# Feed-forward input products as seven block products (Strassen) for pairs of weight pieces

## The chip, the cores and the metric

The kernel runs on one core of a Trainium2 chip. TensorE (PE; PEld is its weight load) multiplies, VectorE (DVE), ScalarE (ACT) and GpSimd (POOL) do the elementwise work, and the queue of SyncE (SP) issues most transfers. The metric is device time in microseconds (us) of one launch, the median of several runs.

## The reference

One step of a two-layer model over 640 tokens (128 of context, 512 latent) with 1024 channels, all in fp32. Each layer has a token-mixing part (attention, neighbourhood attention and a Fourier branch, merged by gates) and a feed-forward part; both are modulated by vectors that come from `c` and `c_ctx`:

```python
mod = silu(c) @ w_ada[l] + b_ada[l]               # 6 x 1024 values: shifts, scales, gates
h = rms_norm(x, g_pre[1]) * (1 + sc2) + sh2       # 640 x 1024
g, u = split(h @ w_ffn_in[l], 2)                  # each 640 x 2816
x = x + g2 * rms_norm((silu(g) * u) @ w_ffn_out[l], g_post[1])
```

## The kernel before

**Products.** Every large product is made of three: each operand is split into a high part, rounded to TensorE's fp32r format, and a low part, the rest; high x high, high x low and low x high are summed in PSUM. The normalised input stands transposed in `hT_hi`, `hT_lo` (channels on partitions, 8 blocks of 128; 640 tokens along the free side).

**Weight pieces.** Weights come in pieces of 512 KB, `[128, 1024]`. A feed-forward input piece (kind `fg` for the gate, `fu` for the other half) holds 128 output channels of all 8 blocks of input channels. `Weights` walks the pieces in the order in which a dry run asked for them: `pump` issues the load of the next piece into one of four `wraw` buffers on SP's queue, `split_next` writes its high part with ACT (`whi`) and its low part with DVE (`wlo`) into one of three slots, and frees the `wraw` buffer.

**Feed-forward.** `ffn` handles the 22 blocks of 128 hidden channels in three parts of 6, 8 and 8 (`FFN_PARTS`). In a part, `proj2` takes each piece for two groups of tokens (384 and 256): 24 matmuls in each, then `evac`. For `fg` ACT takes a tanh and DVE makes `(tanh + 1) * g` in the tile `sg`; for `fu` DVE multiplies, ACT writes the high part into `aT` and DVE the low part. Then `xstat` multiplies `aT` by the output weights (`fo` pieces, 30 matmuls of 512 columns each) and adds into `y`; in the last part `xstat_tiles` does it and finishes one tile of tokens after another.

**Modulation.** The 12 rounds of `w_ada` (a layer, a sixth; 8 pieces of 512 KB each) are spread as a generator, of which `step` takes one tick for every `ada_dt` us of nominal matmul time. In the first layer's token mixing they are small matmuls on TensorE (`wraw,ada_st`, four for a piece). In the feed-forward (`acc` given) each piece is two DVE instructions on 1024 columns, and eight small matmuls with `ones` close a round: six rounds in layer 0 and one in layer 1, with `ADA_DT = 3.0`. `ada_finish` takes all ticks that are left, at once, ahead of the last part's `fo` products.

Each engine works through its own queue in the order in which this code writes it.

Of the kernel before, what the change touches and what calls it, by code (L numbers as in the profile page):

```python
# [69 lines left out]
class Unit:  # L70
    def __init__(self, key):
        self.key = key
        self.raw = self.hi = self.lo = None
        self.done = False


class Weights:
# [41 lines left out]
    def pump(self, bufs=RAW_BUFS):  # L121
        while self.n_dma < len(self.order) and self.n_dma < self.freed + bufs:
            u = self.units[self.order[self.n_dma]]
# [5 lines left out]

    def split_next(self):  # L130
        if self.n_split >= len(self.split):
            return False
# [11 lines left out]
        nc.scalar.activation(hi[:, :u.n], u.raw[:, :u.n], AF.Copy)  # L144
# [1312 lines left out]
```

## Time and profile before

| | us |
|---|---|
| median of 3 runs | 2192.57 (2192.06 to 2193.25) |
| the profiled execution | 2196.1, of which 2194.3 from its first to its last instruction |
| PE busy | 2156.5 (98%) |
| DVE busy | 1131.7 (52%) |
| ACT busy | 790.7 (36%) |
| POOL busy | 354.4 (16%) |

The profiled execution is 3.5 us above the median. A busy PE is not a PE at its peak, since the recorded matmuls overlap; what a matmul costs is read from a stage's time over its count. In the trace, layer 0's feed-forward runs from 645 to 1127 us and layer 1's from 1717 to 2187 us. The input products of their parts are the stretches 645 to 735, 777 to 893, 950 to 1066, and 1717 to 1807, 1849 to 1962, 2018 to 2131 us.

### The profile page before, as it was taken

To read this page: it belongs to the slowest core of one execution; us is meant where nothing else is said; L and a number is where in the kernel's file an instruction comes from. 1 tells how busy PE (TensorE), PEld (TensorE's weight loads), DVE (VectorE), ACT (ScalarE), POOL (GpSimd) and SP (SyncE) were. 2 spreads that over 40 slices of the span, in tenths; PEclk is the share of its full clock that TensorE was granted. 3 is DMA by queue.
4 is the path that set the end of the run, shared out by engine and by line. 5 is a ranking of instruction groups with operands and counts; after the bars stand their busy time and mean duration, and the time that the engine had idled before them with its cause. 6 is when DMAs were issued, how large, how long until landed. Compare 5 with 4: busy or idle time off the path is not lost. (4 is left out here: it accounts for less than half of the span.)

```text
span 2194.3 us, 35177 instructions
## 1 busy us (share of the span) xinstructions
PE 2156.5 (98%) x14260; PEld 2006.2 (91%) x14260; DVE 1131.7 (52%) x2025; ACT 790.7 (36%) x1640; POOL 354.4 (16%) x635
## 2 busy tenths in 40 slices
PE   6999999999999999999999999999999999999998
PEld 3999999998889899899879999999998898998996
DVE  3555565543366566666465556555533662333333
ACT  3644444432253222122256445444433522221221
POOL 2101223322131000000041013233111300000002
PEclk9999999999999999999999999999999999999999
DMA  7311223325634444443332113333124332222221
GB/s 270 109 56 51 63 75 87 83 75 168 237 87 160 136 138 138 146 148 107 107 107 84 49 58 69 82 82 86 60 72 144 108 105 77 77 77 71 74 88 67
DMA packets 250049, 223.78 MB, mean 102 GB/s; under 512 B 10016, under 2 KB 209728, under 8 KB 249632
## 3 DMA queue, kind: packets, MB, share of 16 engines
q1 hardware_dynamic: 243408, 209.60, 30.4%
q0 software_dynamic: 6048, 11.68, 2.6%
q8 instruction: 113, 1.85, 0.3%
q14 instruction: 48, 0.39, 0.1%
q10 hardware_dynamic: 432, 0.25, 0.0%
HBM read 214.91 MB, written 6.59 MB: 101 GB/s over the span
## 5 line engine op out<-in xcount | busy, mean ns | idle before, releaser
L487 PE MATMUL ps_mm<-hT_hi,whi 128*128 128x256 f32 (+1 forms) x2832 | 885.8, 313 | 1.5 <-DVE sg L1098 1.0
L489 PE MATMUL ps_mm<-hT_hi,wlo 128*128 128x256 f32 (+1 forms) x2832 | 877.6, 310 | 0.4 <-DVE wlo L145 0.4
L488 PE MATMUL ps_mm<-hT_lo,whi 128*128 128x256 f32 (+1 forms) x2832 | 877.0, 310 | 0.0
L487 PEld LDWEIGHTS ps_mm<-hT_hi,whi 128*128 128x128 f32 x2832 | 533.3, 188 | 10.7 <-issue 6.0
L489 PEld LDWEIGHTS ps_mm<-hT_hi,wlo 128*128 128x128 f32 x2832 | 533.2, 188 | 0.9 <-DVE wlo L145 0.9
L488 PEld LDWEIGHTS ps_mm<-hT_lo,whi 128*128 128x128 f32 x2832 | 533.3, 188 | 0.6
L145 DVE TENSOR_TENSOR wlo<-wraw,whi 128x1024 fp32r<-128x1024 f32 x253 | 312.8, 1237 | 390.7 <-ACT whi L144 390.1
L144 ACT ACTIVATE whi<-wraw 128x1024 fp32r<-128x1024 f32 x253 | 267.0, 1056 | 274.1 <-PE ps_mm L1138 170.5
L1136 PE MATMUL ps_mm<-whi,aT 128*128 128x512 f32 x400 | 158.5, 396 | 0.0
L1138 PE MATMUL ps_mm<-whi,aT 128*128 128x512 f32 x400 | 157.9, 395 | 0.0
L1137 PE MATMUL ps_mm<-wlo,aT 128*128 128x512 f32 x400 | 157.8, 394 | 0.0
L1272 ACT ACTIVATE aT<-sg 128x384 fp32r<-128x384 f32 x88 | 41.5, 471 | 259.0 <-DVE sg L1270 259.0
L350 DVE SCALAR_TENSOR_TENSOR ada_acc<-ada_raw,ada_st,ada_acc 128x1024 f32<-128x1024 f32 x98 | 123.6, 1279 | 0.0
L487 PE MATMUL ps_mm<-o,whi 128*128 128x256 f32 (+1 forms) x384 | 120.1, 313 | 0.0
L488 PE MATMUL ps_mm<-o,whi 128*128 128x256 f32 (+1 forms) x384 | 118.9, 310 | 0.0
L489 PE MATMUL ps_mm<-o,wlo 128*128 128x256 f32 (+1 forms) x384 | 118.8, 309 | 0.0
L1071 ACT ACTIVATE sg<-ps_mm 128x384 f32<-128x384 f32 x96 | 41.8, 436 | 200.7 <-PE ps_mm L489 200.5
L1266 ACT ACTIVATE sg<-ps_mm 128x384 f32<-128x384 f32 (+1 forms) x88 | 38.6, 438 | 195.1 <-PE ps_mm L489 195.1
L477 POOL TENSOR_SCALAR ss<-ss 128x1 f32<-128x1 f32 x20 | 6.7, 336 | 604.0 <-ACT junk L475 603.3
L1267 DVE SCALAR_TENSOR_TENSOR sg<-sg,ps_mm 128x384 f32<-128x384 f32 (+1 forms) x88 | 42.9, 487 | 104.6 <-ACT sg L1266 104.6
L1099 POOL TENSOR_TENSOR m<-m,sg 128x384 f32<-128x384 f32 x64 | 63.6, 1004 | 196.8 <-DVE sg L1098 196.7
L556 ACT ACTIVATE P<-P,sm 128x384 f32<-128x384 f32 (+2 forms) x160 | 93.0, 586 | 5.4 <-POOL sm L550 5.4
(208 smaller groups left out, 2889.4 us busy)
## 6 DMA issues: line engine op xcount, KB each, us to landing
wraw<-in_w_in SPq DMA_DIRECT2D x92, 512.0 KB, 3.9
wraw<-in_w_ffn_in SPq DMA_DIRECT2D x88, 512.0 KB, 3.7
ada_raw<-in_w_ada SPq DMA_DIRECT2D x56, 512.0 KB, 4.5
wraw<-in_w_ffn_out SPq DMA_DIRECT2D x44, 512.0 KB, 3.5
wraw<-in_w_ada SPq DMA_DIRECT2D x40, 512.0 KB, 4.6
wraw<-in_w_branch SPq DMA_DIRECT2D x24, 512.0 KB, 3.4
wraw<-in_w_out SPq DMA_DIRECT2D x16, 512.0 KB, 3.8
bias<-in_b_rpbT POOLq DMA_DIRECT2D x64, 96.0 KB, 4.0
```

The costliest lines, as they stand in the source:

```text
L144: nc.scalar.activation(hi[:, :u.n], u.raw[:, :u.n], AF.Copy)
L145: nc.vector.tensor_tensor(lo[:, :u.n], u.raw[:, :u.n], hi[:, :u.n].bitcast(F32), op=OP.subtract)
L350: nc.vector.scalar_tensor_tensor(acc[:, s, :], u.raw, c, acc[:, s, :], op0=OP.mult, op1=OP.add)
L487: nc.tensor.matmul(ps, wh, xh[:, c0:c1], start=(k == 0), stop=False)
L488: nc.tensor.matmul(ps, wh, xl[:, c0:c1], start=False, stop=False)
L489: nc.tensor.matmul(ps, wl, xh[:, c0:c1], start=False, stop=(k == K - 1))
L556: nc.scalar.activation(P[:, h, :n], P[:, h, :n], AF.Exp, bias=sm[:, 2 + h:3 + h], accum_out=sm[:, 4 + h:5 + h])
L1099: nc.gpsimd.tensor_tensor(m, m, s, op=OP.add)
L1136: nc.tensor.matmul(ps, xh[:, tc], u.hi[:, i, :], start=st and i == 0, stop=False)
L1137: nc.tensor.matmul(ps, xh[:, tc], u.lo[:, i, :], start=False, stop=False)
L1138: nc.tensor.matmul(ps, xl[:, tc], u.hi[:, i, :], start=False, stop=sp and i == 1)
L1267: nc.vector.scalar_tensor_tensor(t, t, 1.0, ps, op0=OP.add, op1=OP.mult)
```

## The change

**Pairs.** After four single pieces (`FFN_SINGLE = 2` blocks, `fg` and `fu`), two neighbouring pieces of one kind are taken together: 20 pairs in a layer. The pair's weights are four blocks (two pieces a, b by two halves of input channels, 512 columns each), the input four blocks (two halves of 320 tokens by two halves of channels). Instead of eight block products there are seven, of 12 matmuls of 320 columns each, on sums of blocks:

- POOL makes the weight sums, four additions of `[128, 512]` for a pair, partly in the `wraw` buffers. `split_next` then splits seven half pieces of 512 columns instead of two pieces of 1024.
- The input sums S1 to S4 are made once in a layer by `sums`, from the fp32 input that is left in `nt`, while the single pieces run: DVE and POOL add, ACT and DVE split.
- Three of the products go on accumulating in a bank that another product has begun. `pair` copies or adds the parts with ACT, DVE (`tmp<-ps_mm,tmp`) and POOL (`tmp<-tmp`), and calls `evac` for the four results of 320 columns.

**Around it.** The parts become 4, 6, 6 and 6 blocks. Two rounds of modulation, (1, 3) and (1, 4), move from layer 0's feed-forward to TensorE in layer 1's token mixing; four stay, with `ADA_DT = 5.0`. Their accumulator and buffers take the place of `x`, which goes to memory (`xmid`) and comes back ahead of the last part. Some tiles change their place: `y` to `os`, the two extra weight slots to `m0`, `m1`, S2 to `o32`. The tokens in `hT` are reordered (`cut`), so that each half is contiguous.

```diff
-FFN_PARTS = (6, 8, 8)
+FFN_SINGLE = 2
+ADA_MIX = ([(0, 2), (0, 3), (0, 4)], [(1, 3), (1, 4)])
+ADA_FFN = ([(0, 5), (1, 0), (1, 1), (1, 2)], [(1, 5)])
+FFN_PARTS = (4, 6, 6, 6)
+SUMS_AT = (0.1, 0.2, 2.0, 3.0, 4.0, 5.0, 9.0, 99.0)
-ADA_DT, ADA_LAG = 3.0, 3
+ADA_DT, ADA_LAG = 5.0, 3
...
+                if last is None:
+                    self.jobs.append(add)
+                else:
+                    self.jobs.insert(self.jobs.index(("part", last, 3)) + 1, add)
+                self.jobs += [("part", p, 0), ("add4", p)] + [("part", p, i) for i in range(1, 7)]
...
+            add = lambda out, x, y: self.k.nc.gpsimd.tensor_tensor(out, x, y, op=OP.add)
+            if kind == "add":
+                u.c = self.k.fp.tile([128, 1024], F32, name="wadd", tag="wadd", bufs=1)
+                add(u.c[:, h[0]], a0, b0)
+                add(u.c[:, h[1]], u.c[:, h[0]], b1)
+                add(b0, b0, b1)
+            elif kind == "add4":
+                add(a0, u.c[:, h[1]], a1)
...
+                self.split(hi, lo, (a0, c1, c0, a1, b0, b1, a0)[part])
...
+        steps = (lambda: within(a22, a21, a22, OP.subtract), lambda: across(a21, a11, a21),
+                 lambda: store("S1", a22, "m1"), lambda: across(a11, a22, a11),
+                 lambda: store("S2", a11, "o32"), lambda: within(a12, a12, a11, OP.add),
+                 lambda: store("S3", a21, "m0"), lambda: store("S4", a12, None))
+        for dt, f in zip(offsets, steps):
+            self.defer(dt, f, "sums")
...
+        def product(i, ps, first, last):
+            w, x = W.part(a, b, i), self.left[i]()
+            for k in range(4):
+                for j, (p, q) in enumerate(((0, 0), (0, 1), (1, 0))):
+                    nc.tensor.matmul(ps, w[p][:, k, :], x[q][:, k, :], start=first and k == 0 and j == 0,
+                                     stop=last and k == 3 and j == 2, skip_group_check=True)
+
+        def end(i):
+            W.part_done(a, b, i)
+            self.step(12 * 320 * PE_COL)
...
+        product(0, p1, True, False)
+        nc.scalar.activation(m1, p1, AF.Copy)
+        end(0)
+        p2 = psum()
+        product(1, p2, True, False)
+        nc.vector.tensor_tensor(u2, p2, m1, op=OP.add)
+        end(1)
+        p3 = psum()
+        product(2, p3, True, False)
+        nc.scalar.activation(m5, p3, AF.Copy)
+        end(2)
+        product(3, p1, False, True)
+        evac(0, p1, 0)
+        end(3)
+        product(4, p2, False, True)
+        nc.vector.tensor_tensor(u3, p2, m1, op=OP.add)
+        nc.gpsimd.tensor_tensor(m5, m5, u3, op=OP.subtract)
+        end(4)
+        product(5, p3, False, True)
+        nc.vector.tensor_tensor(u2, p3, u2, op=OP.subtract)
+        evac(1, u2, 0)
+        end(5)
+        p4 = psum()
+        product(6, p4, True, True)
+        nc.vector.tensor_tensor(m1, p4, u3, op=OP.add)
+        evac(0, m1, 1)
+        evac(1, m5, 1)
+        end(6)
...
-        if l == 0:
-            self.ada = self.ada_rounds([(0, 2), (0, 3), (0, 4)])
-            self.ada_acc, self.ada_dt = 0.0, ADA_D0
+        self.ada = self.ada_rounds(ADA_MIX[l])
+        self.ada_acc, self.ada_dt = 0.0, ADA_D0
...
+                side = self.fp.tile([128, 5, D], F32, name="ada_side", tag="x", bufs=1)
+                self.W.side_open([side[:, i, :] for i in range(2, 5)], 8 * len(rounds))
...
                 self.ada_finish()
-                self.alt_pieces("os")
+                self.alt_pieces()
                 gm = self.load_gm(l, 1)
+                self.x = self.fp.tile([128, 5, D], F32, name="x", tag="x", bufs=1)
+                for t in range(5):
+                    nc.sync.dma_start(self.x[:, t, :], self.xmid[t * 128:t * 128 + 128])
```

First place, DVE's queue in layer 0's second part, at the pieces of kind `fu`. Before: `wlo` is the low part of a whole piece, `ada_acc` an instruction of the modulation, `sg` and `aT` are `evac`.

```order
L1270 TENSOR_TENSOR sg_7791<-sg_7791,ps_mm_7830 128x384
L1273 SCALAR_TENSOR_TENSOR aT2_7764<-sg_7791,aT0_7762 128x384
L350 SCALAR_TENSOR_TENSOR ada_acc_6894<-ada_raw_6895,ada_st_76,ada_acc_6894 128x1024
L1270 TENSOR_TENSOR sg_7791<-sg_7791,ps_mm_7860 128x256
L1273 SCALAR_TENSOR_TENSOR aT2_7764<-sg_7791,aT0_7762 128x256
L145 TENSOR_TENSOR wlo_7889<-wraw_7673,whi_7888 128x1024
```

The same queue now, in the middle of a `fu` pair of the second part, from the addition after product 1 (the second of the seven) to the one after product 5.

```order
L703 TENSOR_TENSOR tmp_6548<-ps_mm_8516,tmp_6548 128x320
L165 TENSOR_TENSOR wlo2_256<-wraw_8379,whi2_255 128x512
L165 TENSOR_TENSOR wlo2_256<-wadd_8452,whi2_255 128x512
L1485 TENSOR_TENSOR sg_8430<-sg_8430,ps_mm_8494 128x320
L1488 SCALAR_TENSOR_TENSOR aT1_8361<-sg_8430,aT0_8360 128x320
L165 TENSOR_TENSOR wlo1_254<-wadd_8452,whi1_253 128x512
L449 SCALAR_TENSOR_TENSOR ada_side_6873<-ada_side_6873,ada_st_76 128x1024
L713 TENSOR_TENSOR tmp_6548<-ps_mm_8516,tmp_6548 128x320
L165 TENSOR_TENSOR wlo1_254<-wraw_8379,whi1_253 128x512
L717 TENSOR_TENSOR tmp_6548<-ps_mm_8533,tmp_6548 128x320
```

Between two additions that TensorE waits for stand half-piece splits, `evac` and the modulation (`ada_side` in the place of `ada_acc`). POOL had nothing in these stretches but the start of a modulation round; now its queue holds this for each pair, the three sums of the next pair, the fourth one (`add4`), and the subtraction of `pair`:

```order
L201 TENSOR_TENSOR wadd_7404<-wraw_7332,wraw_7334 128x512
L201 TENSOR_TENSOR wadd_7404<-wadd_7404,wraw_7334 128x512
L201 TENSOR_TENSOR wraw_7334<-wraw_7334 128x512
L201 TENSOR_TENSOR wraw_7332<-wadd_7404,wraw_7332 128x512
L714 TENSOR_TENSOR tmp_6548<-tmp_6548 128x320
```

Second place, PE's queue where the last modulation round of layer 0's feed-forward is closed (`ones`). Before, it stands between the two groups of one input piece of the last part:

```order
L488 MATMUL ps_mm<-hT_lo,whi 128x384
L489 MATMUL ps_mm<-hT_hi,wlo 128x384
L362 MATMUL ps_t<-ada_acc,ones 32x256 x8
L487 MATMUL ps_mm<-hT_hi,whi 128x256
L488 MATMUL ps_mm<-hT_lo,whi 128x256
```

Now it stands behind the last pair and ahead of all `fo` products of the last part:

```order
L690 MATMUL ps_mm<-hT_lo,whi_253 128x320
L690 MATMUL ps_mm<-hT_hi,wlo_254 128x320
L461 MATMUL ps_t<-ada_side,ones 32x256 x8
L1346 MATMUL ps_mm<-whi_251,aT_9412 128x512
L1347 MATMUL ps_mm<-wlo_252,aT_9412 128x512
```

DVE's queue at that place, where nine instructions of the modulation now follow one another behind the last pair's `evac`:

```order
L1485 TENSOR_TENSOR sg<-sg,tmp 128x320
L1488 SCALAR_TENSOR_TENSOR aT_9414<-sg,aT_9414 128x320
L449 SCALAR_TENSOR_TENSOR ada_side<-ada_side,ada_st 128x1024 x9
L463 TENSOR_TENSOR ada_m<-ps_t,ada_m 128x256
L465 TENSOR_TENSOR ada_m<-ada_m,ada_g 128x256
```

What moved is the end of the round: with fewer nominal microseconds ahead of the last part and a tick every 5.0 instead of 3.0, `ada_finish` has ticks left to take.

More of the change, by code (lines that the diff above doesn't have):

```diff
@@ L121, in pump @@
     def pump(self, bufs=RAW_BUFS):
[L122 to L123 removed]
+        while self.n_dma < len(self.loads) and self.n_dma < self.freed + bufs:
+            u = self.units[self.loads[self.n_dma]]
             u.raw = self.k.fix.tile([128, 1024], F32, name="wraw", tag="wraw", bufs=RAW_BUFS)
@@ L128, in pump, with split, open_slots @@
             self.n_dma += 1
+    def split(self, hi, lo, src):
+        self.k.nc.scalar.activation(hi, src, AF.Copy)
+        self.k.nc.vector.tensor_tensor(lo, src, hi.bitcast(F32), op=OP.subtract)
+    def open_slots(self):
+        fix = self.k.fix
+        self.slots = [tuple(fix.tile([128, 1024], F32R, name=f"{n}{i}") for n in ("whi", "wlo")) for i in range(SPLIT_BUFS)]
+        self.idle = [(i, h) for i in range(SPLIT_BUFS) for h in range(2)]
     def split_next(self):
-        if self.n_split >= len(self.split):
+        if self.n_job >= len(self.jobs):
@@ L153, in free, with record @@
+        self.n_job += 1
+        return True
+    def free(self, n):
+        self.freed += n
         self.pump()
+    def record(self, e):
+        for key in e[1:] if e[0] == "pair" else (e,):
+            assert key not in self.units
+            u = self.units[key] = Unit(key)
+            u.hi = u.lo = u.raw = Null()
+        (self.side if self.is_side(e) else self.order).append(e)
     def get(self, key):
@@ L170, in get, with part @@
         return u
+    def part(self, a, b, i):
+        if self.recording:
+            if i == 0:
+                self.record(("pair", a, b))
+            return Null(), Null()
+        p = self.pairs[a, b]
+        self.pump()
+        while p.parts[i] is None:
+            assert self.split_next(), (a, b, i)
+        self.split_all()
+        return p.parts[i][1]
     def split_all(self):
@@ L179, in early, with part_done @@
             self.get(key)
+    def part_done(self, a, b, i):
+        if not self.recording:
+            self.idle.append(self.pairs[a, b].parts[i][0])
+            self.split_all()
     def done(self, u):
-        u.done = True
         if self.recording:
@@ L1288, in ffn @@
-                self.ada = self.ada_rounds(rounds, acc)
+                        self.proj((l, kind, n), g, evac(kind, n), 4, HALVES)
+                self.W.alt.clear()
+                for kind, n in seq[3:]:
+                    self.proj2((l, kind, n), evac(kind, n), HALVES)
+                self.run_tasks(("sums",))
+                rounds = ADA_FFN[l]
+                self.run_tasks(range(5))
+                side = self.fp.tile([128, 5, D], F32, name="ada_side", tag="x", bufs=1)
+                self.W.side_open([side[:, i, :] for i in range(2, 5)], 8 * len(rounds))
@@ L1289, in ffn @@
+                self.ada = self.ada_rounds(rounds, side[:, 0:2, :])
                 self.ada_acc, self.ada_dt = 0.0, ADA_DT
-            for kind, n in seq:
-                self.proj2((l, kind, n), evac(kind, n))
+            for n in range(first, n0 + nt, 2):
+                for kind in ("fg", "fu"):
+                    ev = [evac(kind, n + i) for i in range(2)]
+                    self.pair((l, kind, n), (l, kind, n + 1), lambda i, src, g: ev[i](src, g))
             if p == 0:
-                self.W.alt.clear()
-                y = self.fix.tile([128, 5, D], F32, name="y", tag="m", bufs=1)
+                y = self.fix.tile([128, 5, D], F32, name="y", tag="os", bufs=1)
```

276 lines of the change are left out of this document (182 added, 94 removed).

## The prediction, made before the changed kernel ran

> **What bounds the kernel now.** I read the page first (busy time, chain), then the stages of the two feed-forwards as windows, then single rows for prices.
>
> ```profile
> span 2194.3 us, 35177 instructions
> PE 2156.5 (98%) x14260; PEld 2006.2 (91%) x14260; DVE 1131.7 (52%) x2025; ACT 790.7 (36%) x1640; POOL 354.4 (16%) x635
> PE ps_mm L487 11%; PE ps_mm L488 11%; PE ps_mm L489 11%; PE ps_mm L1136 3%; PE ps_mm L1138 3%; PE ps_mm L1137 3%; PE ps_o L586 1%; PE ps_t L573 1%; PE ps_s L546 1%; PE ps_s L547 1%; POOL hT_lo L468 0%; PE ps_mm L1050 0%; PE ps_mm L1051 0%; PE ps_mm L1049 0%; PE ps_s L1007 0%
> ```
>
> PE is busy all along, and its matmuls lead the chain. So a matmul less is worth its whole issue interval, as long as the other engines keep up. The windows (columns: stretch, length, busy time and count of each engine in the order PE, PEld, DVE, ACT, POOL, then granted clock) give that interval and the room beside it:
>
> ```profile
> 504.90:585.30 80.40, 80.40 (x628) 68.36 (x629) 22.12 (x38) 19.94 (x35) 15.25 (x23) 1.00 0.64 211
> 1593.60:1657.30 63.70, 63.70 (x433) 63.70 (x434) 22.11 (x34) 19.36 (x35) 11.86 (x12) 1.00 0.21 67
> ...
> 950.00:1066.00 116.00, 116.00 (x806) 114.33 (x805) 75.87 (x97) 29.49 (x47) 1.11 (x2) 1.00 0.36 116
> ...
> 2018.00:2131.00 113.00, 113.00 (x769) 113.00 (x768) 42.90 (x63) 29.51 (x47) 0.00 (x0) 1.00 0.25 75
> ```
>
> Layer 1's last input stage takes 113.0 us for 768 matmuls of 384 and 256 columns: 0.147 us each, so for their mean, 320. PE never waits there; DVE is busy 38% of it, and in layer 0, with the modulation, 65%. POOL is idle.
>
> **TensorE's terms.** A pair has 84 matmuls of 320 columns instead of 96 of that mean: 12 x 0.147 = 1.76 us less, 12.35 instead of 14.1. For 40 pairs that is **-70.6 us**. Two modulation rounds move to layer 1's token mixing. The first two rows above are the same 432 products in layer 0, with 24 modulation pieces, and in layer 1, with none: 16.7 us more, 0.70 us a piece, so 16 pieces cost **+11.1**. In layer 0's feed-forward their closing matmuls go: the third row is 3 us longer than the fourth for some 2.5 rounds, 1.2 each, **-2.4**. Nothing covers these three, since PE is full there.
>
> **What it adds beside TensorE, and whether it stays beside.** Prices:
>
> ```profile
> L145 DVE TENSOR_TENSOR wlo<-wraw,whi 128x1024 fp32r<-128x1024 f32 x253 | 312.8, 1237 | 390.7 <-ACT whi L144 390.1
> L144 ACT ACTIVATE whi<-wraw 128x1024 fp32r<-128x1024 f32 x253 | 267.0, 1056 | 274.1 <-PE ps_mm L1138 170.5 <-PE ps_mm L488 40.6 <-DMA wraw<-in_w_in 28.9
> L350 DVE SCALAR_TENSOR_TENSOR ada_acc<-ada_raw,ada_st,ada_acc 128x1024 f32<-128x1024 f32 x98 | 123.6, 1279 | 0.0
> L1270 DVE TENSOR_TENSOR sg<-sg,ps_mm 128x384 f32<-128x384 f32 x44 | 24.4, 554 | 50.8 <-PE ps_mm L489 50.8
> L1270 DVE TENSOR_TENSOR sg<-sg,ps_mm 128x256 f32<-128x256 f32 x44 | 18.5, 420 | 29.4 <-PE ps_mm L489 29.4
> L1273 DVE SCALAR_TENSOR_TENSOR aT<-sg,aT 128x384 fp32r<-128x384 f32 x44 | 24.6, 559 | 26.0 <-ACT aT L1272 26.0
> L1273 DVE SCALAR_TENSOR_TENSOR aT<-sg,aT 128x256 fp32r<-128x256 f32 x44 | 18.7, 425 | 21.3 <-ACT aT L1272 21.3
> L617 POOL TENSOR_TENSOR rot<-rot,ca 128x256 f32<-128x256 f32 x20 | 14.8, 742 | 116.1 <-ACT rot L615 116.1
> L1318 POOL TENSOR_TENSOR y<-y,gm 128x512 f32<-128x512 f32 x10 | 13.3, 1340 | 0.6
> ```
>
> And four stretches of the timeline (start, length), DVE and POOL in turn:
>
> ```profile
> 630.85 1.78 DVE L468 TENSOR_TENSOR hT_lo<-nt,hT_hi 128x512 fp32r<-128x512 f32 x1
> ...
> 643.16 1.27 DVE L1212 SCALAR_TENSOR_TENSOR x<-nt,ss,x 128x1024 f32<-128x1024 f32 x1
> 644.35 0.68 DVE L468 TENSOR_TENSOR hT_lo<-nt,hT_hi 128x512 fp32r<-128x512 f32 x1
> 644.95 2.35 DVE L145 TENSOR_TENSOR wlo<-wraw,whi 128x1024 fp32r<-128x1024 f32 x2
> ...
> 657.87 0.54 DVE L1270 TENSOR_TENSOR sg<-sg,ps_mm 128x384 f32<-128x384 f32 x1
> 659.00 0.56 DVE L1273 SCALAR_TENSOR_TENSOR aT<-sg,aT 128x384 fp32r<-128x384 f32 x1 [0.59 <-ACT aT L1272]
> ```
>
> ```profile
> 630.30 1.78 POOL L468 TENSOR_TENSOR hT_lo<-nt,hT_hi 128x512 fp32r<-128x512 f32 x1 [0.16 <-ACT hT_hi L467]
> ...
> 643.98 4.45 POOL L468 TENSOR_TENSOR hT_lo<-nt,hT_hi 128x512 fp32r<-128x512 f32 x1 [1.94 <-ACT hT_hi L467]
> ```
>
> These rows show three things. Back to back, DVE starts its next instruction 0.08 us before the last one's recorded end (644.35 + 0.68 against 644.95). A DVE instruction with two inputs in SBUF and a POOL one exclude each other: DVE's split takes 0.68 alone and 1.78 beside POOL's, ending 0.55 after POOL's end (632.08); POOL's addition of 512 columns takes 4.45 when DVE has four such instructions in a row, and ends at 648.43, 1.13 after DVE's (647.30). So POOL holds what they share for 1.13 us, and less in proportion for 320 columns, some 0.73 (estimate from 742 ns at 256 columns). And a low part waits 0.59 us for ACT's high part.
>
> The Trainium skill ("SBUF — State Buffer", section "SBUF: two separate sides") says that whoever starts first gets the shared pair "for the whole instruction". By that, POOL's ten instructions for two pairs would shut DVE out for their whole recorded 12.5 us instead of 10.5, and the sum below would be some 13 us higher; the measured 0.55 and 1.13 are below the recorded lengths, so the trace agrees on the lock and not on its length.
>
> DVE, for a `fg` and a `fu` pair together (24.7 us of PE): 14 half splits x 0.60 = 8.4; 8 additions of `pair` and 12 `evac` instructions of 320 columns x (0.49 - 0.08) = 8.2; six places where it must wait for ACT between two of them, 0.54 for 320 columns and the 0.08 of overlap lost, = 3.7. That is 20.3. In layer 0 come 3.8 of the modulation (22.4 nominal us / 5.0, 16 of 19 ticks) x 1.2 = 4.5: 24.8. POOL holds 8 x 1.13 + 2 x 0.73 = 10.5 us. Of these, 4 us can lie beside DVE instructions that read PSUM (ten of 0.41; L617 always runs beside one and keeps its 742 ns) and 3.7 in DVE's waits for ACT, so between 2.8 and 10.5 come on top. I take 4, nearer the low end, because POOL gets its turn in just those places. Two pairs then take DVE 24.3 us in layer 1, which PE's 24.7 covers, and 28.8 in layer 0: **4.1 us more than PE**. ACT, 14 half splits x 0.55 + 12 x 0.45 = 13 us of 24.7, stays hidden.
>
> PE notices when product 4 writes the bank that DVE's addition after product 1 reads: DVE may be two products late, 3.5 us, less that addition: 3.0. Parts 1 to 3 have three such double pairs; up to the sixth pair's addition DVE falls two doubles and a quarter behind, 2 x 4.1 + 1, so PE waits 6.2 us a part, 18.6 in all. The first part has one double, behind the input sums: 4. Layer 0: **+23**. With 2.8 and 10.5 instead of 4 it is 13 and 74, and layer 1 adds 0 and 30.
>
> The input sums, in DVE's queue up to the first pair's addition: 6 instructions of 1024 columns x 1.15, 10 of 256 x 0.34, 8 of `evac` x 0.41 and 7 half splits x 0.60 are 18 us; with 4 of waits for ACT, 4 of POOL's sums and 1.5 until POOL has left the input, 27.5. PE takes 24.7 from the second group of the single pieces to product 4 (168 matmuls). **+3** in each layer (0 to 8). One round in layer 1's first parts: **+2**.
>
> The flush: the last round of layer 0 now ends in nine modulation instructions on DVE, 9 x 1.2 = 10.8 us, behind the last `evac` (five instructions and two waits, 3.3, and 2 of lag), and PE's closing matmuls stand ahead of all `fo` products. PE waits 16 us. Its clock then starts low, as here, after a gap of the same kind:
>
> ```profile
> 1126.51 0.39 PE L1138 MATMUL ps_mm<-whi,aT 128*128 128x512 f32 x1
> 1127.32 0.44 PE L487 MATMUL ps_mm<-hT_hi,walt 128*128 128x384 f32 x1 [0.42 <-ACT hT_hi L467]
> 1128.92 0.44 PE L488 MATMUL ps_mm<-hT_lo,walt 128*128 128x384 f32 x1 [1.16 <-DVE hT_lo L468]
> ...
> 1130.33 0.53 PE L487 MATMUL ps_mm<-hT_hi,walt 128*128 128x384 f32 x1
> 1130.64 0.53 PE L488 MATMUL ps_mm<-hT_lo,walt 128*128 128x384 f32 x1
> ...
> 1132.57 0.44 PE L488 MATMUL ps_mm<-hT_lo,walt 128*128 128x384 f32 x1
> 1132.85 0.34 PE L489 MATMUL ps_mm<-hT_hi,walt 128*128 128x384 f32 x1
> ```
>
> Starts are 0.31 us apart instead of 0.18 (384 columns at the interval above), from 1129.4 to 1132.6: 1.6 lost. Flush: **+18** (14 to 20).
>
> Costed at nothing: the loads (a pair's two pieces and a modulation piece, 1.5 MB in 12 us, about the 116 GB/s of the third window); `x` to memory and back on SP's queue, behind `gm` and ahead of the last pieces, 20 us before it is read; a third pass over `y`, since DVE has room in `xstat`. POOL's sums are issued five products (8.8 us) ahead of their use; a load that comes later than that is paid in full.
>
> **Sum:** -70.6 + 11.1 - 2.4 + 23 + 6 + 2 + 18 = -12.9. On the profiled execution's 2196.1 that is 2183; against the median, 3.5 us lower, **2180**.
>
> **Rivals.**
> - *The others keep up.* DVE never falls 3 us behind, because lag dies out in each `fo` stage: -70.6 + 8.7 + 2 + 14 = -46, 2147. For it: DVE's 20.3 against 24.7. Against: 24.8 in layer 0 without any POOL. 0.21.
> - *The shared access bounds both feed-forwards; slower.* If 7.5 of POOL's 10.5 us stay uncovered, two pairs take DVE 32.3 and 27.8 us: PE waits 46 and 12, and the sum is -70.6 + 8.7 + 58 + 8 + 18 = +22, 2215. It decides from 5.8 us on, where the sum is zero. For it: the 4.45 us row, POOL starved while DVE is dense; against: POOL's results are needed five products later. 0.22.
> - *The clock.* Each wait of a few us lets the clock fall, as after 1126.5, where PE had stood 1.6 us in two pieces: some 11 waits x 1.6 = +18, 2198. The Trainium skill ("TensorE: Matmul & The Clock Gate", "What's actually happening") puts the fall after one idle window of about 3.4 us; by that rule shorter waits cost nothing and the sum stays, but the rows show a loss after shorter ones. 0.13.
>
> **Chances.** The forecast has 0.44. About 0.2%, 4.4 us, is what a measurement here can tell from no change. Faster: 0.21 + 0.40 of the forecast + 0.01 = 0.62; same 0.08, from the forecast and the clock; slower 0.22 + 0.08 = 0.30. The range reaches from near the first rival, 2142, to past the second, 2218; beyond lie POOL's full 10.5 us and luck. The forecast alone: 2165 to 2190.
>
> **What the profile after would show.** 480 fewer input matmuls at 0.147 us; layer 1's token mixing 11 us longer; in layer 0's pairs PE waiting for the additions of `pair` and DVE busy over 90%, in layer 1's hardly a wait; one gap of some 16 us on PE ahead of layer 0's last `fo` stage, ended by DVE; POOL's additions far above 1.3 us. The prediction is wrong if PE's gaps in layer 1's pairs pass 10 us, if layer 0's stay under 10 or pass 45, or if the gap ahead of `fo` is missing.

## The result: slower by 2.3%, and the profile after

| | us |
|---|---|
| changed kernel, median of 4 runs | 2243.24 (2243.17 to 2245.34) |
| kernel before, beside it, 4 runs | 2192.91 (2192.06 to 2194.38) |
| ratio | 1.0231, 95% interval 1.0213 to 1.0249 |

The change costs 50 us where a gain of 13 was forecast. From the page of the changed kernel: the busy times, the chain by engine, and three of its costliest groups (busy time, mean ns of one, then the idle time of the engine just ahead and what ended it). L690 is the matmul in `pair`, L699 ACT's copy of product 0, L201 POOL's weight sums.

```profile
span 2241.4 us, 35680 instructions
PE 2123.7 (95%) x13876; PEld 1958.2 (87%) x13876; DVE 1366.4 (61%) x2397; ACT 908.0 (41%) x1944; POOL 667.0 (30%) x847
PE 51%; DVE 11%; ACT 4%; issue 3%; POOL 1%; DMA 1%; ACTq 0%; DVEq 0%; POOLq 0%
L690 PE MATMUL ps_mm<-hT_hi,whi 128*128 128x320 f32 x640 | 204.2, 319 | 39.6 <-ACT tmp L699 39.6
L690 PE MATMUL ps_mm<-S,whi 128*128 128x320 f32 x960 | 219.3, 317 | 3.1 <-DVE tmp L703 3.1
L201 POOL TENSOR_TENSOR wraw<-wadd,wraw 128x512 f32<-128x512 f32 x40 | 64.8, 1620 | 232.2 <-DVE wlo L165 141.5
```

PE has 384 matmuls fewer on balance (14260 before, 13876 now), but it is busy only 95% of the span instead of 98%. It waits 39.6 us for ACT's copy, the addition that I had watched (L703) costs 3.1. Stages, first of the changed kernel (columns: stretch, length, busy time and count of PE, PEld, DVE, ACT, POOL, then granted clock, DMA share, GB/s), then two of the kernel before:

```profile
640.50:680.20 39.70, 32.81 (x210) 31.43 (x209) 31.32 (x43) 18.27 (x36) 22.94 (x21) 0.96 0.31 106
...
864.70:950.90 86.20, 79.37 (x524) 77.77 (x523) 75.59 (x109) 35.89 (x73) 35.57 (x28) 0.96 0.35 110
...
1986.60:2067.10 80.50, 76.15 (x506) 75.58 (x505) 61.98 (x95) 36.17 (x74) 33.30 (x23) 0.98 0.28 86
2108.70:2190.80 82.10, 77.51 (x506) 76.97 (x505) 62.25 (x95) 35.95 (x74) 33.29 (x23) 0.96 0.27 84
...
1080.00:1097.20 17.20, 2.06 (x16) 0.43 (x16) 14.49 (x17) 4.25 (x6) 0.65 (x1) 0.62 0.28 91
1097.20:1150.20 53.00, 47.85 (x202) 38.52 (x199) 26.01 (x34) 16.04 (x35) 15.53 (x23) 0.90 0.44 149
1150.20:1162.00 11.80, 0.97 (x8) 0.58 (x6) 8.67 (x14) 6.45 (x14) 3.15 (x4) 0.74 0.44 131
1162.00:1699.60 537.60, 535.33 (x3939) 509.71 (x3940) 276.08 (x629) 232.60 (x546) 120.27 (x233) 1.00 0.30 86
```

```profile
1065.80:1126.90 61.10, 58.78 (x267) 47.38 (x265) 31.35 (x41) 24.62 (x50) 19.68 (x26) 1.00 0.32 104
1127.30:1653.90 526.60, 523.48 (x3807) 506.00 (x3808) 282.69 (x633) 235.61 (x550) 121.04 (x228) 1.00 0.27 75
```

A part of six pairs has 504 matmuls, 74.1 us at 0.147. The second row is layer 0's third part, rows three and four are layer 1's last two, which hold no modulation: they too take 80.5 and 82.1, and DVE is busy only 77 and 76% of them. The first row is layer 0's 192 matmuls of single pieces, 28.2 us at that price. The fifth row is the flush, the next two are layer 0's last `fo` stage (180 matmuls, 42 us where nothing waits) and a gap behind it, the last is layer 1's token mixing, 11.0 longer than in the row of the kernel before.

From the starts of the matmuls in the pairs (intervals above 0.45 us are waits, those from 0.18 to 0.45 low clock, each less 0.147) and the lengths of the stages, the difference of the two spans, 47.1 us, comes out as

| us | layer 0 | layer 1 |
|---|---|---|
| 240 matmuls fewer x 0.147 | -35.3 | -35.3 |
| PE's waits in the pairs | +24.3 | +20.7 |
| low clock behind them | +11.9 | +10.1 |
| single pieces | +7 | +6 |
| flush | +15.9 | |
| last `fo` stage and the start of the next mixing | +17.3 | |
| two modulation rounds on PE | | +11.0 |
| up to the end of layer 0's `wo` stage | -4.3 | |

These come to +49.3; with the forecast's -2.4 for the closing matmuls, which were not measured by themselves, and 1.0 more at the end of the program it is 47.9. (Single pieces: 39.7 and 39.0 against 28.2, less the 4.6 and 4.5 by which the first input stage before was above its price. Last `fo` stage: 53.0 - 42.0 + 11.8, less 61.1 - 56.0 + 0.4 before.)

Now one wait, in layer 1's third part, in the timeline (start, length): PE, ACT, POOL and DVE in turn. The products are numbered 0 to 6 as in the code. Product 5 of an `fu` pair ends at 2038.2, product 6 at 2040.0; products 0, 1 and 2 of the next pair follow, and the last row of PE is its product 3.

```profile
2045.09 0.31 PE L690 MATMUL ps_mm<-S,wlo 128*128 128x320 f32 x1
2047.44 0.41 PE L690 MATMUL ps_mm<-hT_hi,whi 128*128 128x320 f32 x1 [2.04 <-ACT tmp L699]
```

```profile
2046.08 0.47 ACT L1487 ACTIVATE aT<-sg 128x320 fp32r<-128x320 f32 x1 [0.96 <-DVE sg L1485]
2046.45 0.61 ACT L164 ACTIVATE whi<-wraw 128x512 fp32r<-128x512 f32 x1
2046.98 0.42 ACT L699 ACTIVATE tmp<-ps_mm 128x320 f32<-128x320 f32 x1
```

```profile
2038.84 1.28 POOL L201 TENSOR_TENSOR wadd<-wraw 128x512 f32<-128x512 f32 x1
2040.20 1.44 POOL L201 TENSOR_TENSOR wadd<-wadd,wraw 128x512 f32<-128x512 f32 x1
2041.60 1.54 POOL L201 TENSOR_TENSOR wraw<-wraw 128x512 f32<-128x512 f32 x1
```

```profile
2038.41 0.49 DVE L717 TENSOR_TENSOR tmp<-ps_mm,tmp 128x320 f32<-128x320 f32 x1 [0.28 <-PE ps_mm L690]
2038.93 1.54 DVE L1485 TENSOR_TENSOR sg<-sg,tmp 128x320 f32<-128x320 f32 x1
2041.01 0.98 DVE L1488 SCALAR_TENSOR_TENSOR aT<-sg,aT 128x320 fp32r<-128x320 f32 x1 [0.54 <-ACT aT L1487]
2041.91 1.78 DVE L165 TENSOR_TENSOR wlo<-wraw,whi 128x512 fp32r<-128x512 f32 x1
2043.61 0.48 DVE L722 TENSOR_TENSOR tmp<-ps_mm,tmp 128x320 f32<-128x320 f32 x1
2044.12 0.49 DVE L1485 TENSOR_TENSOR sg<-sg,tmp 128x320 f32<-128x320 f32 x1
2045.15 0.49 DVE L1488 SCALAR_TENSOR_TENSOR aT<-sg,aT 128x320 fp32r<-128x320 f32 x1 [0.54 <-ACT aT L1487]
2045.56 0.48 DVE L1485 TENSOR_TENSOR sg<-sg,tmp 128x320 f32<-128x320 f32 x1
```

Product 3 goes on in the bank of product 0, so it must wait until ACT has copied product 0 (L699). In ACT's queue that copy stands behind the high parts of the last two `evac` calls of the pair before, and these wait for DVE, call by call. DVE begins on time at 2038.41. POOL's three sums stretch its next three instructions by 1.05, 0.49 and 1.10, to 1.54, 0.98 and 1.78. With 0.49, 0.49 and 0.68 instead, and all behind them earlier by as much, the copy would end at 2044.8, an estimate from these rows; PE is due at 2045.24, one interval behind the last matmul of product 2. So DVE and ACT, one after the other, need 6.35 us from the start of L717 to the end of the copy, and PE gives them 6.83: the slack is 0.5, and the sums take 2.6.

### The profile page after: what moved, and what is told of

Same layout as the page of the kernel before. It is cut to its first block, busy times and chain, and to the rows that moved or that the text cites. A ratio compares the mean times of both kernels' runs of the same rounds, so it can differ in the third digit from the quotient of the medians.

```text
span 2241.4 us, 35680 instructions
## 1 busy us (share of the span) xinstructions
PE 2123.7 (95%) x13876; PEld 1958.2 (87%) x13876; DVE 1366.4 (61%) x2397; ACT 908.0 (41%) x1944; POOL 667.0 (30%) x847
## 4 chain that ended last, share of the span: by engine, by line
PE 51%; DVE 11%; ACT 4%; issue 3%; POOL 1%; DMA 1%; ACTq 0%; DVEq 0%; POOLq 0%
PE ps_mm L690 14%; PE ps_mm L596 6%; PE ps_mm L598 6%; PE ps_mm L597 6%; PE ps_mm L1348 5%; PE ps_mm L1346 5%; PE ps_mm L1347 4%; DVE wlo L165 3%; DVE sg L1485 2%; PE ps_o L798 1%; PE ps_t L785 1%; ACT whi L164 1%; DVE ada_side L449 1%; ACT aT L1487 1%; DVE x L1423 1%
## 5 line engine op out<-in xcount | busy, mean ns | idle before, releaser
L165 DVE TENSOR_TENSOR wlo<-wraw,whi 128x512 fp32r<-128x512 f32 (+1 forms) x373 | 381.3, 1025 | 305.7 <-ACT whi L164 302.3
L596 PE MATMUL ps_mm<-hT_hi,whi 128*128 128x256 f32 (+2 forms) x1552 | 489.1, 315 | 1.9 <-DVE sg L1309 1.0
L598 PE MATMUL ps_mm<-hT_hi,wlo 128*128 128x256 f32 (+2 forms) x1552 | 480.8, 310 | 2.0 <-DVE wlo L165 2.0
L597 PE MATMUL ps_mm<-hT_lo,whi 128*128 128x256 f32 (+2 forms) x1552 | 480.3, 309 | 0.0
L164 ACT ACTIVATE whi<-wraw 128x512 fp32r<-128x512 f32 (+1 forms) x373 | 304.3, 825 | 258.4 <-PE ps_mm L1348 87.3
L596 PEld LDWEIGHTS ps_mm<-hT_hi,whi 128*128 128x128 f32 x1552 | 292.4, 188 | 11.8 <-issue 7.6
L690 PE MATMUL ps_mm<-hT_hi,whi 128*128 128x320 f32 x640 | 204.2, 319 | 39.6 <-ACT tmp L699 39.6
L690 PE MATMUL ps_mm<-S,whi 128*128 128x320 f32 x960 | 219.3, 317 | 3.1 <-DVE tmp L703 3.1
L690 PE MATMUL ps_mm<-hT_hi,wlo 128*128 128x320 f32 x640 | 202.9, 317 | 0.0
L690 PE MATMUL ps_mm<-hT_lo,whi 128*128 128x320 f32 x640 | 202.6, 317 | 0.0
L690 PEld LDWEIGHTS ps_mm<-S,whi 128*128 128x128 f32 x960 | 166.3, 195 | 5.8 <-DVE tmp L703 4.4
L690 PEld LDWEIGHTS ps_mm<-hT_hi,whi 128*128 128x128 f32 x640 | 124.0, 194 | 44.7 <-ACT tmp L699 44.3
L690 PE MATMUL ps_mm<-S,wlo 128*128 128x320 f32 x480 | 150.6, 314 | 0.0
L201 POOL TENSOR_TENSOR wraw<-wadd,wraw 128x512 f32<-128x512 f32 x40 | 64.8, 1620 | 232.2 <-DVE wlo L165 141.5
L690 PEld LDWEIGHTS ps_mm<-hT_hi,wlo 128*128 128x128 f32 x640 | 124.8, 195 | 0.0
L690 PEld LDWEIGHTS ps_mm<-hT_lo,whi 128*128 128x128 f32 x640 | 124.4, 194 | 0.3
```

Source lines behind the costliest of these rows:

```text
L164: self.k.nc.scalar.activation(hi, src, AF.Copy)
L165: self.k.nc.vector.tensor_tensor(lo, src, hi.bitcast(F32), op=OP.subtract)
L201: add = lambda out, x, y: self.k.nc.gpsimd.tensor_tensor(out, x, y, op=OP.add)
L596: nc.tensor.matmul(ps, wh, xh[:, c0:c1], start=(k == 0), stop=False)
L597: nc.tensor.matmul(ps, wh, xl[:, c0:c1], start=False, stop=False)
L598: nc.tensor.matmul(ps, wl, xh[:, c0:c1], start=False, stop=(k == K - 1))
```

## The experiments

All ratios are against the kernel before on the same chip. The expectations of e2, e5 and e9 count the products from 1 (their product 6 is the code's 5); theories are named by letters: A and E, the chain at a pair's end and its short slack; C, sheer amount on DVE; D, the place of the sums.

**e1, no weight sums.** The kernel leaves POOL's sums out.

```diff
-                add(u.c[:, h[0]], a0, b0)
-                add(u.c[:, h[1]], u.c[:, h[0]], b1)
-                add(b0, b0, b1)
-                add(a0, u.c[:, h[1]], a1)
-                self.split(hi, lo, (a0, c1, c0, a1, b0, b1, a0)[part])
+                self.split(hi, lo, (a0, b1, b0, a1, b0, b1, a0)[part])
```

> Left out: POOL's four weight sums of every pair; the splits read the plain half pieces instead, the same number and size. Theory A (a chain at a pair's end): the pairs lose some 31 us a layer because POOL's additions stretch DVE's instructions behind product 5 of an fu pair, so that ACT's copy of the next pair's first product comes late and PE stands before its fourth product. Then nearly all of the pairs' waits and most of their low clock go: 45 us less than the changed kernel, 2198 (2185 to 2208), with under 8 us of waits in layer 1's pairs. Rival B (the chain is too long by itself, POOL or not): the waits before the fourth product go on at half their size, 2225. Rival C (DVE's sheer load): DVE gains some 8 us of 24.7 a double pair, so the time is as with A, but e2 then gains nothing.

Measured: 2177.14, ratio 0.9929 (0.9914 to 0.9944). 66 us go, more than any theory gave. The stretches of its third part in layer 0 and in layer 1:

```profile
848.70:926.90 78.20, 76.35 (x523) 74.51 (x522) 65.00 (x109) 36.30 (x73) 9.61 (x11) 1.00 0.38 121
...
1934.80:2008.70 73.90, 73.90 (x506) 73.88 (x505) 53.36 (x95) 36.35 (x73) 7.93 (x6) 1.00 0.30 94
```

Layer 1's part takes 73.9, with no wait; that is the forecast price of 0.147 a matmul. DVE is busy 53.4 there instead of 62.0: 24 sums on POOL cost it 8.6, or 2.9 for a `fg` and a `fu` pair. Layer 0, with the modulation and without the sums, loses 4. Rival B, a chain too long by itself, falls; A and C both stand. Of the 66 us some 6 lie in the single pieces (36.1 instead of 39.7 and 39.0), where the first pair's sums had stood in POOL's queue ahead of the last tile's norm, and 9 in the first pairs (24.6 in each layer, with no wait, instead of 28.2 and 29.7).

**e8, the same instructions with an eighth of the columns**, but for the first pair of a layer, which keeps its full sums. The rest of each sum is left out.

```diff
-            add = lambda out, x, y: self.k.nc.gpsimd.tensor_tensor(out, x, y, op=OP.add)
+            add = lambda out, x, y: self.k.nc.gpsimd.tensor_tensor(out[:, 0:n], x[:, 0:n], y[:, 0:n], op=OP.add)
```

> Left out: seven eighths of each weight sum (64 of 512 columns are added, but for the first pair of a layer); the instructions, their order and who waits for them are as in the changed kernel. If it is the time for which POOL keeps DVE out: as without the sums, 2180 (2176 to 2190). If it is that splits on ACT and DVE stand in their queues for a sum that is not ready: above 2215.

Measured: 2187.38, 0.9971 (0.9962 to 0.9981). 56 of the 66 us go with the length of the sums; their order and semaphores cost little. The other 10 are about what the first pairs' full sums cost: single pieces and first pair together take 65.4 and 66.2 us here and 60.7 in e1. Short sums are also ready sooner, but in the changed kernel no wait of ACT or DVE in the feed-forward ends at a sum. So what the length costs is the time for which POOL keeps DVE out.

**e2, the last two `evac` calls behind ACT's next copy.**

```diff
         nc.scalar.activation(m1, p1, AF.Copy)
+        self.late_evac()
         end(0)
...
-        evac(0, m1, 1)
-        evac(1, m5, 1)
+        self.late = [lambda: evac(0, m1, 1), lambda: evac(1, m5, 1)]
```

> All work kept; the last two evac calls of a pair are issued behind ACT's copy of the next pair's first product, so that this copy no longer stands behind them in ACT's queue. Theory A: the 40 us in which PE waits for that copy before a fourth product go, and their low clock with them: 40 us less than the changed kernel, 2203 (2190 to 2215). Rival C (DVE and POOL are simply too slow for TensorE): the waits go over to the addition after product 2, which PE meets before the fifth product, and the time stays within 8 us of 2243.

Measured: 2236.8, 1.0204 (1.0187 to 1.0221): 6 us, where A gave 40. PE's waits in layer 1's last two parts, in the changed kernel and then here (us in total, times, longest):

```profile
PE ps_mm L690 <- ACT tmp L699: 8.9, 4, 2.3
```

```profile
PE ps_mm L690 <- DVE tmp L704: 6.2, 4, 1.7
```

The wait went over to DVE's addition after product 1 (L704 here), which now stood behind the moved calls. This spoke for C.

**e9, the same calls behind that addition too**, so that nothing PE meets soon stands behind them.

```diff
         nc.vector.tensor_tensor(u2, p2, m1, op=OP.add)
+        self.late_evac()
         end(1)
```

> All work kept; the last two evac calls of a pair come behind both ACT's copy of the next pair's first product and DVE's addition after its second. Theory E (slack): from DVE's addition behind product 6 to the end of that copy the two engines need 6.5 us one after the other, of the 7.0 that TensorE takes, so DVE may be 0.5 us late and not 3; now it may be some 3.5 late. Then layer 1's waits in its last two parts (4.7 and 4.9 us) go to nearly 0, and both layers lose half or more of the rest: 2207 (2198 to 2216). Rival C (amount: an fu pair alone has more for DVE than its 12.35 us of TensorE): the waits move to another product, as when only the copy was moved: 2236 (2230 to 2242).

Measured: 2231.3, 1.0167 (1.0148 to 1.0185), inside C's range. By layers it reads otherwise. In layer 1's last two parts this is left of the 8.9 us of waits, and no low clock (76.3 and 76.2 us instead of 80.5 and 82.1):

```profile
PE ps_mm L690 <- ACT tmp L708: 2.3, 4, 1.0
PE ps_mm L690 <- DVE tmp L703: 0.7, 2, 0.3
```

Layer 0's third part only goes from 86.2 to 83.4.

**e10, the steps of the two calls taken in turn, one round less on DVE, the first sums later.**

```diff
+        for fs in zip(*self.late):
+            for f in fs:
+                f()
...
-ADA_MIX = ([(0, 2), (0, 3), (0, 4)], [(1, 3), (1, 4)])
-ADA_FFN = ([(0, 5), (1, 0), (1, 1), (1, 2)], [(1, 5)])
+ADA_MIX = ([(0, 2), (0, 3), (0, 4)], [(1, 2), (1, 3), (1, 4)])
+ADA_FFN = ([(0, 5), (1, 0), (1, 1)], [(1, 5)])
```

> The same, with the two calls' steps taken in turn (one wait of DVE for ACT less in an fu pair, 0.54), modulation round (1, 2) on TensorE in layer 1's token mixing (+5.6, and no flush, -17), and the first pair's sums behind the last tile's norm (-3.5 in each layer). Against the run with the evac calls moved alone: -20. So 2187 with theory E, 2216 with rival C.

Measured: 2197.99, 1.0017 (1.0008 to 1.0027): 45 us less than the changed kernel, between the two forecasts and nearer E's. Its third part in layer 0 and in layer 1:

```profile
866.40:947.80 81.40, 76.84 (x524) 74.68 (x524) 75.58 (x108) 35.27 (x73) 34.65 (x28) 1.00 0.38 116
1956.50:2030.40 73.90, 73.90 (x506) 73.89 (x505) 62.48 (x95) 35.71 (x73) 33.72 (x23) 1.00 0.31 94
```

The second row settles layer 1's last two parts, which hold no modulation. POOL and DVE do there what they did in the changed kernel, 33.7 and 62.5 us against 33.3 and 62.0, and PE waits for nothing. What was missing was slack at one place, not time on DVE. In layer 0 the modulation adds 13 us to DVE's busy time, and its 75.6 us leave it no room beside the 74.1 that PE's products take. Layer 1's second part, with its one round, still takes 82.6 us, with DVE busy for 72.5. The later first sums gained nothing: the single pieces are 3 us shorter, but single pieces and first pair together take 68.9 and 68.1 us, as in e9 (69.7 and 68.0).

**e11, all modulation of the feed-forwards on TensorE**, the four rounds of layer 0 and the one of layer 1 (`ada_rounds` without an accumulator, into the second PSUM tag).

```diff
-                self.ada = self.ada_rounds(rounds, side[:, 0:2, :])
+                self.ada = self.ada_rounds(rounds)
```

> The same as the run before, but all five modulation rounds of the two feed-forwards go to TensorE where they stand (four matmuls a piece, 40 pieces of 0.70 = +28, instead of two DVE instructions), and round (1, 2) stays in layer 0. DVE then has in layer 0 what it has in layer 1. If amount is what layer 0's waits come from, its parts get as short as layer 1's, 75 to 80 us, and the run is level with the one before or some us faster, 2186; if the modulation does not matter, it is 22 slower.

Measured: 2190.77, 0.9989 (0.9980 to 0.9999). Layer 0's second part:

```profile
743.10:823.30 80.20, 80.20 (x573) 75.36 (x570) 63.31 (x97) 37.24 (x76) 35.12 (x28) 1.00 0.46 140
```

It now has no wait: the 6.1 above its 74.1 are its eight and a half modulation pieces at 0.7 (68 matmuls in the trace, eight for a piece). Layer 1's second part falls from 82.6 to 75.8. So what e10 leaves in these parts comes from the modulation on a DVE that the sums had filled, and 40 pieces on PE are 7 us cheaper than 32 on DVE and 8 on PE. Whether each part's share is sheer amount, or also where the modulation stands in DVE's queue, was not separated: e1 still lost 4 us in layer 0's part with DVE busy for only 65.0. What is left in the pairs of e11 is one wait of 6.3 us in each layer's first pair.

**e5 and e6, the sums elsewhere.** POOL first reads a column of ACT's copy, and the next pair's sums follow; e6 also moves round (1, 2) and the first pair's sums as e10 does.

```diff
         nc.scalar.activation(m1, p1, AF.Copy)
+        nc.gpsimd.tensor_scalar(mark[:, 0:1], m1[:, 0:1], EPS, None, op0=OP.add)
...
+                self.jobs += [("part", p, 0), add, ("add4", p)] + [("part", p, i) for i in range(1, 7)]
```

> All work kept. POOL's sums of the next pair are moved in its queue behind a one-column instruction that reads ACT's copy of the present pair's first product, so that they run while TensorE does products 2 to 4 and no longer products 6 and 7, where DVE and ACT finish the pair. Theory D (place: the sums hit DVE in the one stretch whose work TensorE meets soonest): the waits in layer 1's pairs fall from some 21 us to under 6, their low clock goes, and so in layer 0: 35 to 45 less than the changed kernel, 2203 (2195 to 2212). Rival C (amount: DVE loses the same 3 us a double pair wherever the sums lie): within 8 us of 2243.

> The same, and besides: modulation round (1, 2) goes to TensorE in layer 1's token mixing too (8 pieces of 0.70, +5.6), so that layer 0 has three rounds on DVE and no flush (-17); and the first pair's sums wait in POOL's queue until the last tile's norm has passed (-3 in each layer, from the wait of 3.6 us at its transposes). Against the run with the sums moved alone: -17, to 2186 (2178 to 2195) with theory D; with rival C 2226.

Measured: 2251.57, 1.0265 (1.0250 to 1.0281), and 2234.6, 1.0187 (1.0172 to 1.0202). D fails: the waits took another form. Waits of ACT from layer 1's second part on in e5, of a kind that the changed kernel does not have (L160 is the split, L197 the sum):

```profile
ACT whi L160 <- POOL wadd L197: 30.3, 13, 3.3
```

Now the splits stand in ACT's queue for a sum that is not there yet, and what is behind them waits too. e6 takes 17 us less than e5, as expected in sum, but not from the terms expected: the first sums give nothing (single pieces and first pair take 66.5 us in each layer of e5, 66.6 and 67.3 in e6), while layer 0's last part is 4.5 us shorter.

**e7, the sums on DVE.**

```diff
-            add = lambda out, x, y: self.k.nc.gpsimd.tensor_tensor(out, x, y, op=OP.add)
+            add = lambda out, x, y: self.k.nc.vector.tensor_tensor(out, x, y, op=OP.add)
```

> All work kept; DVE makes the weight sums instead of POOL, 24 of 0.60 us in a part of six pairs = 14.4, where POOL's cost DVE 8.6 (62.0 against 53.4 us busy without them). In layer 1 DVE then has 67.8 of 73.8 us, in layer 0 with the modulation 79. Rival C (amount): layer 0 loses another 6 us a part and layer 1 too has some more waits, 2265. Theory D (place and single long holds): layer 1's waits shrink to some 10, since three additions of 0.60 stand in the chain instead of 2.6 us of stretching, layer 0's stay: 2230.

Measured: 2247.67, 1.0248 (1.0233 to 1.0264), between the two. Its third part in layer 1:

```profile
1987.10:2071.60 84.50, 77.91 (x506) 77.12 (x505) 65.84 (x112) 35.73 (x74) 7.90 (x6) 0.96 0.27 82
```

DVE is busy 12.5 more than without sums, POOL's had cost it 8.6: POOL was not the wrong engine by amount.

**e3, no flush.**

```diff
-ADA_DT, ADA_LAG = 5.0, 3
+ADA_DT, ADA_LAG = 4.2, 3
```

> ADA_DT 4.2 instead of 5.0: layer 0's last modulation round closes among the pairs, as before the change, and nothing is left to flush ahead of its last fo stage. If the flush costs only its own gap: 17 us less, 1 to 3 more for DVE's denser queue, 2228 (2224 to 2232), and PE still waits some 11 us where layer 1's token mixing begins. If that later wait and the low clock in the last fo stage are the flush's backlog, another 18 go: 2210.

Measured: 2246.3, 1.0245 (1.0230 to 1.0261). The flush's gap is gone, and its 17 us are paid in the pairs, where the same instructions now stand closer: layer 0's parts take 92.3, 93.4 and 91.6 instead of 85.8, 86.2 and 87.4. The wait where layer 1 begins is still 11 us, so it was not the flush's backlog.

**e4, the kernel before with a last part of 6.**

```diff
-FFN_PARTS = (6, 8, 8)
+FFN_PARTS = (8, 8, 6)
```

> The kernel before, with its parts as 8, 8 and 6 blocks instead of 6, 8 and 8 (and the two extra weight slots set to the last part's new pieces); no pairs. If a shorter last fo stage no longer hides the tails of the tiles (scaling, residual, norm, transposes, splits, which go on at the same pace): PE waits 10 to 18 us in that stage of layer 0 and where layer 1 begins, 2208 (2202 to 2212). If the waits of the changed kernel there come from the flush or from the reload of x, which this kernel does not have: within 3 us of the kernel before, 2193.

Measured: 2207.59, 1.0067 (1.0052 to 1.0082). PE in the changed kernel and then in e4, at a tile's transposes and at layer 1's first products:

```profile
1141.68 1.97 PE L548 MATMUL ps_t<-ident,y 128*128 128x128 f32 x8 [5.15 <-ACT y L557]
...
1162.00 0.69 PE L596 MATMUL ps_mm<-hT_hi,walt 128*128 128x384 f32 x1 [10.83 <-ACT hT_hi L576]
```

```profile
1119.43 1.97 PE L449 MATMUL ps_t<-ident,y 128*128 128x128 f32 x8 [5.25 <-ACT y L458]
...
1139.76 0.69 PE L487 MATMUL ps_mm<-hT_hi,walt 128*128 128x384 f32 x1 [10.31 <-ACT hT_hi L467]
```

The same two waits, without pairs, flush or reload: 15 us are the price of the shorter last part alone.

**e12, the best of these**: e11, with the first pair's sums behind the input sums.

```diff
+                self.jobs += [("part", p, 0)] + [add] * (last is None) + [("add4", p)] + [("part", p, i) for i in range(1, 7)]
```

> As the run with the modulation on TensorE (2190.8), but the first pair's sums stand in POOL's queue behind the input sums, after the first half piece of that pair, instead of just ahead of them. There the single pieces and the first pair took 34.7 + 34.7 us in each layer, of which 10 are a wait of 6.6 us for ACT's copy and its low clock, since POOL's weight sums run into the input sums on DVE. In the run in which the sums were moved the same two stretches took 34.7 + 32.1 with the short slack. If it is this collision: 3 to 5 us less in each layer, 2183 (2180 to 2187), faster than the kernel before. If the input sums are too long by themselves: 2190.

Measured: 2189.77, 0.9985 (0.9976 to 0.9994), 1 us better than e11 and not 8. With e11 it is the only version that keeps all work and is ahead of the kernel before, by 2 and 3 us, hardly more than can be told apart. The single pieces and the first pair still take 36.3 + 33.7 us:

```profile
640.40:676.70 36.30, 32.77 (x211) 31.60 (x210) 30.41 (x41) 17.34 (x36) 21.07 (x19) 0.95 0.42 145
676.50:710.20 33.70, 28.75 (x187) 27.28 (x186) 24.30 (x36) 14.46 (x27) 12.41 (x13) 0.90 0.33 110
```

So the place of the first sums was not what holds that stretch. The time is the one given for input sums that are too long by themselves, but e1, which keeps them and leaves the weight sums out, takes 36.1 + 24.6 there: it takes both. Whether a thinner set of input sums would help was not tried.

## Why the prediction was wrong

**The step that failed** is the one behind the "+23" and layer 1's 0: "PE notices when product 4 writes the bank that DVE's addition after product 1 reads: DVE may be two products late, 3.5 us, less that addition: 3.0". Two things were wrong in it. There is an earlier meeting, product 3 and ACT's copy, and what stands ahead of that copy in ACT's queue hangs on DVE through three round trips; the slack is 0.5. And I compared DVE with PE over a `fg` and a `fu` pair together, where DVE's work is bunched at the end of the `fu` pair, in which POOL's sums fell. e9 and e10 show it: the same work with more slack leaves no wait in layer 1's last two parts. e2 alone had not shown it, since it moved the calls ahead of the next meeting.

Of the 60 us between the forecast's sum and the trace (-12.9 and +47.1), 14 are waits in the pairs (45.0 for 23 + 6 + 2), 22 the low clock behind them, 13 the single pieces, and 15 the flush and the last `fo` stage (33.2 for 18); the 4 us by which layer 0's `wo` stage ends sooner go the other way. So the step that failed stands behind at most some 36 of them; the others are terms that the sum did not have.

**What was right.** The matmul's price (e1, 73.9 us for 504), the modulation on PE (+11.0 for +11.1), the flush (a stretch of 17.2 us with 2.1 of PE in it, for 18), and the share of POOL's hold that DVE pays, "I take 4": 2.9 by e1. The input sums' +3 is right in size: at the first pair PE waits 2.0 us in layer 0 and 3.5 in layer 1. But there too it waits for ACT's copy ahead of product 3, and without the weight sums (e1) not at all.

**Right in size for the wrong reason.** Layer 0's waits, 24.3 for 23 and the input sums' 3, but DVE was not "over 90%" busy, it had 88% of 86.2 us. Layer 1's last two parts, with 77 and 76%, were to have hardly a wait; the profile puts 4.3 and 4.6 us there, against 6.8 in layer 0's third part. By its own tests the prediction fell there: layer 1's waits passed 10 us.

**Terms left out.** The low clock behind waits in the pairs, 22 us: I had it as a rival (18) and counted it only behind the flush, so that the 23 us of waits which the forecast itself had in layer 0 cost no clock. 11.9 of the 22 lie in layer 0. The shorter last part, +17 in the trace and 15 by e4: the change was read for what it adds to the pairs, and the `fo` stage, in which five tiles' norms must hide, became 14 us shorter without a term. The single pieces, +13: POOL's queue, in which the first pair's sums pass the last tile's norm, is 3 in each layer, though moving them (e10 to e12) only carried the wait over to the first pair. In e1 the single pieces still are 3.3 us longer than the same matmuls before the change (36.1 - 28.2 = 7.9 against 4.6): PE waits 1.9 us for ACT's high part of the last tile's norm, at the first product of the second half of the tokens, and the clock falls. The flush's cure, e3, gained nothing, so the flush was a price of layer 0's full DVE and not only of its place.

**The rivals.** "Shared access bounds both feed-forwards" was nearest in time, and e1 and e8 confirm that POOL's hold sets the waits; but its price, 7.5 of 10.5 uncovered, was 2.9, and e10 shows that it does not bound layer 1's last two parts. That it came nearest is in part luck: it had neither the low clock in the pairs nor the shorter last part. "The others keep up" needed e10's order, and then held only where no modulation is on DVE.

**Open.** Why the changed kernel reaches the end of layer 0's `wo` stage 4.3 us sooner is not known; e4, which is the kernel before up to there, is 2.8 us sooner too, so most of it may be the one execution that was profiled, 3.5 us above its median. The closing matmuls' -2.4 was not measured by itself.

## What to carry to other kernels

When a change loads an engine beside TensorE, do not compare sums over a period: follow, for each matmul that reuses a bank or a buffer, the chain of queue neighbours on every engine up to it, and take the shortest slack. In layer 1's last two parts a few instructions moved out of that chain (e9, e10) took away every wait, with the same work on the same engines. And when a stage is cut shorter, ask what it was hiding.

## What the runs showed of the hardware

**The clock falls after short waits, but not after each.** PE's waits in the pairs of the twelve traces that have pairs, by the length of the wait, and how often at least eight matmuls at the low clock followed: 1.0 to 1.6 us, 0 of 25; 1.6 to 2.0, 4 of 27; 2.0 to 2.7, 17 of 32; 2.7 to 3.2, 11 of 17; 3.2 to 4.0, 13 of 14; longer, 24 of 24. Up to 3.2 us a fall costs 1.6 us, 14 matmuls that start 0.267 apart. Two waits of almost the same length, in the changed kernel and in e6:

```profile
1893.02 0.62 PE L690 MATMUL ps_mm<-hT_hi,whi 128*128 128x320 f32 x1 [3.28 <-ACT tmp L699]
1893.44 0.47 PE L690 MATMUL ps_mm<-hT_lo,whi 128*128 128x320 f32 x1
```

```profile
891.95 0.56 PE L688 MATMUL ps_mm<-S,whi 128*128 128x320 f32 x2 [2.97 <-DVE tmp L703]
892.35 0.30 PE L688 MATMUL ps_mm<-S,wlo 128*128 128x320 f32 x1
```

Starts are 0.27 apart after the first and 0.147 after the second. The granted clock tells the two apart. In all fourteen traces its changes lie on a grid of 3.413 us, and what it does in one window of the grid follows from the window before. These are the two windows around each wait, of the changed kernel and then of e6 (columns as above):

```profile
1889.65:1893.06 3.41, 0.13 (x2) 0.04 (x1) 2.31 (x5) 1.88 (x5) 0.19 (x1) 1.00 0.00 0
1893.06:1896.48 3.42, 3.42 (x13) 3.42 (x14) 3.42 (x6) 1.79 (x4) 0.17 (x1) 0.50 0.52 154
```

```profile
886.95:890.36 3.41, 2.03 (x12) 1.76 (x12) 3.26 (x3) 1.31 (x3) 3.22 (x3) 1.00 0.51 144
890.36:893.77 3.41, 1.82 (x12) 1.82 (x13) 3.41 (x5) 0.63 (x1) 2.72 (x3) 1.00 0.87 234
```

The first wait lies almost whole in one window, and the next window is low. The second is cut by an edge of the grid into 1.5 and 1.6 us, and the clock stays. The twelve traces with pairs have 286 windows at full clock in which PE waits in a pair (a start more than 0.45 us behind the last one, less 0.147). Where it stood for less than 1.9 us of the window, the next one was low in 0 of 212; from 1.9 to 2.0 us, in 7 of 10; for longer, in 64 of 64. The Trainium skill ("TensorE: Matmul & The Clock Gate", "What's actually happening") has the fall after at least one idle window of about 3.4 us on a grid that runs by itself. The trace agrees on the grid and its length; but the window need not be idle throughout, since 2.0 of its 3.4 us were always enough here and less than 1.9 never. So whether a wait of 2 to 4 us costs clock is a matter of where it lies in the grid.

**A sum on POOL costs DVE less than its hold.** Alone, POOL holds DVE for 1.13 us of an addition of 512 columns, as the prediction read; among DVE's other work 24 of them cost DVE 8.6 us of busy time, 0.36 each (e1), less than the 0.52 each that DVE's own additions took (e7, 12.5 of 24). In layer 1's last two parts they cost time only by where they fall (e10, with the same sums, has no wait there); in layer 0's third part, where DVE is busy for 75.6 us beside PE's 74.1 (e10), there is no room for the 0.36 us either.
